# Twenty-eight key tiles turned beside the even layer: each load, its turning passes and its store pinned to one projection unit

## The chip, the cores and the metric

The kernel runs on one core of one Trainium2 chip. The metric is the device time of one execution in microseconds (us). The engines named below are TensorE (PE: matmuls; PEld: its weight loads), VectorE (DVE), ScalarE (ACT), GpSimd (POOL) and SyncE (SP). SP computes nothing: it issues nearly all transfers (DMAs), one after the other, in the order of its queue, and holds the queue while an issue waits for a semaphore.

## The reference, cut to what matters

One inference step of two layers, for a prompt of 2048 tokens and for 8 sample sequences of 4 tokens, each with 2048 cached tokens in pages of 128 rows:

```python
def even_mixer(h, w_in, ...):
    proj = h @ w_in                                   # all of the even layer's projections
    qa, fa, ia, ga, qb, kb, vb, gb, fb = _split(proj, ...)
    o_a, s_a = gated_linear_chunked(...)              # HGRN2 heads (group A)
    o_b = fox_attend(hb(qb), kb_h, vb_h, log_fb)      # forgetting attention (group B)
    return jnp.concatenate([o_a * silu(ga), o_b * silu(gb)], -1) @ w_out, ...

def fox_sample(q, k, v, log_f, k_pages, v_pages, logf_pages, page_table):
    k_past = k_pages[page_table].reshape(db, -1, H, dh)    # 128 pages of 128 x 4 x 128, f32
    logit_past = einsum('bthd,bshd->bhts', q, k_past) * scale + ...
    ...
```

The odd layer (GLA) and a final norm follow. `logit_past` needs the cached keys with the head dimension on the partitions, so every key page has to be turned before TensorE can use it.

## The kernel before, in words

The even layer is one long run of 32 projection units, `us[0]` to `us[31]`: 16 blocks of columns of `w_in` for the first half of the prompt, and the same 16 for the second half. A unit is a chain of matmuls (L629 to L631: each product is done as three f16 matmuls of high and low parts), the eviction of the results by ScalarE and VectorE, and stores by SP. Beside the units run four linear-attention heads per half (`lin(h)`, tiles `qA`, `kA`, `gl_A`). `staged` walks through a unit's steps, and prepares the weights of the units one to three ahead: load (`wr_...`), largest absolute value (`rm_...`, L306), scale (`pow_...`, `kc`), split in f16 parts (`w_...`, L360).

At the second and the fourth step of a unit (`n in (1, 3)`), `staged` calls `beside(2 * j + n // 2)`, and that calls `ahead`. `ahead` prepares `PRE = 28` of the 32 tiles of cached keys. A tile takes:

- four loads of 256 KB, `kp<-in_cache_fox_k`, L1528 on SP, ahead of which SP reads the four page numbers into registers (L1520: a TENSOR_LOAD and eight short instructions);
- four turning passes of VectorE, `kT<-kp`, L1532, STREAM_TRANSPOSE of 128x512 f32;
- one store of 1 MB, `kT<-kT`, L1548 on SP, into a scratch tensor in DRAM.

The last four tiles are turned later, in the fox phase, which also reads the 28 back (`ktd<-kT`, L1592) for the scores of the samples (`sc`, L1692). The fox phase follows the 32 units directly: its first VectorE instruction is L1418 (`L<-s,cm`).

The order on each engine is not the order of this code. The program is recorded, and a scheduler then puts each engine's instructions in a row by its own timetable: an instruction that has its inputs and its buffer by that timetable may stand far ahead of where it is written. A block `with tc.issue_after(ins)` adds an edge: whatever is recorded in it for the engine of `ins` stands behind `ins` in that engine's row. Edges set only the row; on the chip every engine works through its row strictly, and waits at an instruction until its semaphores are there. In the kernel before, a tile's loads have an edge to the loads of the tile before (`last_page`), and the turning passes have none.

Tile buffers: `lr` (two) up to unit 15, `wr` (three, shared with raw weights) from then on. Each tile uses one for `kp` and one for the turned tile.

## Time and profile before

| | |
|---|---|
| median of 3 runs | 2357.52 us (2351.48 to 2358.5) |
| profiled execution | 2351.95 us; its span (first to last instruction) 2350.3 us |
| busy, share of the span | PE 95%, PEld 67%, DVE 59%, ACT 42%, POOL 31% |
| mean granted TensorE clock | 0.978 |
| turning passes L1532 in the even layer | 112, from 45.7 to 639.3 us, 70.2 us busy |
| fox phase's first L1418 on VectorE | 936.3 us |

The span is 1.65 us shorter than the profiled execution's time, and that execution is 5.6 us under the median. "Granted clock" is the share of TensorE's full speed that the chip gave in a stretch; the records show 1.0 and 0.5 in turns, and a row gives the mean. DMA share is the mean busy share of 16 DMA engines and can be a little over 1. "Idle before" in a row is the time the engine stood still just ahead of these instructions, and the name behind the arrow is what ended it.

### The profile page before, as it was taken

The numbers are of one execution on the slowest core, as the hardware profiler recorded it, in microseconds if no ns is written. First come the engines' busy times: TensorE is split into PE (matmuls) and PEld (weight loads), VectorE is DVE, ScalarE is ACT, GpSimd is POOL, SyncE is SP. The second block draws the span as 40 slices with busy tenths as digits, with TensorE's granted clock in tenths as the row PEclk, the third lists the DMA queues.
The fourth block names the chain that finished last, engine by engine and source line by source line (L and its number), as shares of the span: only waits on it lengthen the run. The fifth ranks groups of instructions, "written<-read, shape, count | busy, mean of one in ns | idle before, by whom it ended". The sixth has DMA issues, their size and how long they took to land.

```text
span 2350.3 us, 58071 instructions
## 1 busy us (share of the span) xinstructions
PE 2221.6 (95%) x23316; PEld 1581.5 (67%) x23316; DVE 1395.6 (59%) x3138; ACT 992.1 (42%) x2200; POOL 731.1 (31%) x788
## 2 busy tenths in 40 slices
PE   6988999899899999898999999999999999999998
PEld 5556767785365578564545888777677666666887
DVE  5865566843654455758677635356665655547554
ACT  5322434411022122546566543546545535545343
POOL 1232234200110111524345536144452432322233
PEclk9999999999899999999999999999999999999999
DMA  8878335899954135998784978523233532115554
GB/s 220 257 217 271 110 101 173 275 283 271 281 163 145 60 124 158 353 321 234 236 271 154 325 223 253 144 91 109 80 118 76 129 103 63 44 60 162 162 182 157
DMA packets 367600, 420.65 MB, mean 179 GB/s; under 512 B 108785, under 2 KB 303666, under 8 KB 356066
## 3 DMA queue, kind: packets, MB, share of 16 engines
q1 hardware_dynamic: 365186, 410.32, 57.3%
q0 software_dynamic: 2144, 6.62, 0.8%
q8 instruction: 183, 3.00, 0.5%
q14 instruction: 87, 0.71, 0.1%
HBM read 274.16 MB, written 125.78 MB: 170 GB/s over the span
## 4 chain that ended last, share of the span: by engine, by line
PE 46%; DVE 4%; DMA 2%; ACT 2%; issue 2%; POOL 2%; SPq 1%; POOLq 0%; DVEq 0%; ACTq 0%
PE pt_o L629 4%; PE pt_o L630 4%; PE pt_o L631 4%; PE pt L1454 2%; PE pt_Cv L631 2%; PE pt_Cv L629 2%; PE pt_Cv L630 2%; PE pv L1772 1%; PE o_C L913 1%; PE fo L629 1%; PE gl_C L760 1%; PE fo L630 1%; PE fo L631 1%; PE s L629 1%; PE sc L1692 1%
## 5 line engine op out<-in xcount | busy, mean ns | idle before, releaser
L629 PE MATMUL pt_o<-w_o,act 128*128 128x256 f16 x1024 | 278.9, 273 | 1.1 <-ACT sg1C L686 1.1
L630 PE MATMUL pt_o<-w_o,act 128*128 128x256 f16 x1024 | 278.9, 273 | 0.0
L631 PE MATMUL pt_o<-w_o,act 128*128 128x256 f16 x1024 | 278.7, 273 | 0.0
L629 PEld LDWEIGHTS <-act 128*128 128x128 f16 x2304 | 227.4, 99 | 41.8 <-DVE Bvs L1074 6.0
L630 PEld LDWEIGHTS <-act 128*128 128x128 f16 x2304 | 227.4, 99 | 34.4 <-issue 4.7
L631 PEld LDWEIGHTS <-act 128*128 128x128 f16 x2304 | 227.2, 99 | 30.9 <-issue 2.0
L793 POOL TENSOR_TENSOR kA<-kA,fA 128x512 f32<-128x512 f32 (+1 forms) x56 | 76.6, 1368 | 404.7 <-PE gl_A L760 323.0
L629 PE MATMUL pt_Cv<-w_Cv,act 128*128 128x256 f16 (+1 forms) x512 | 141.4, 276 | 0.0
L631 PE MATMUL pt_Cv<-w_Cv,act 128*128 128x256 f16 (+1 forms) x512 | 141.3, 276 | 0.0
L630 PE MATMUL pt_Cv<-w_Cv,act 128*128 128x256 f16 (+1 forms) x512 | 141.2, 276 | 0.0
L1426 ACT ACTIVATE L<-L,nm,kc 128x512 f32<-128x512 f32 (+3 forms) x160 | 118.2, 740 | 44.8 <-DVE nm L1424 42.7
L1532 DVE STREAM_TRANSPOSE kT<-kp 128x512 f32<-128x512 f32 x112 | 70.2, 681 | 105.8 <-DMA kp<-in_cache_fox_k 99.3
L1461 ACT ACTIVATE th<-pt 128x512 f16<-128x512 f32 (+3 forms) x159 | 81.0, 527 | 110.2 <-PE pt L1454 109.3
L1434 POOL TENSOR_SCALAR L<-L,nm 128x512 f32<-128x512 f32 (+3 forms) x160 | 100.3, 642 | 86.8 <-DVE nm L1430 45.2
L793 POOL TENSOR_TENSOR kC<-kC,fC 128x512 f32<-128x512 f32 (+1 forms) x56 | 80.4, 1437 | 139.7 <-PE gl_C L760 94.1
L1462 DVE TENSOR_TENSOR tl<-pt,th 128x512 f16<-128x512 f32 (+3 forms) x159 | 94.7, 607 | 27.8 <-ACT th L1461 25.9
L1454 PE MATMUL pt<-ident,L 128*128 128x128 f32 x544 | 89.3, 278 | 4.4 <-DVE tl L1462 2.6
L1454 PEld LDWEIGHTS pt<-ident,L 128*128 128x128 f32 x544 | 64.4, 142 | 32.5 <-DVE tl L1462 9.8
L792 DVE TENSOR_TENSOR qC<-qC,fC 128x512 f32<-128x512 f32 (+1 forms) x56 | 72.9, 1302 | 22.0 <-PE gl_C L760 22.0
L1972 ACT ACTIVATE vC<-pt_Cv,kc 128x512 f32<-128x512 f32 (+1 forms) x40 | 23.9, 599 | 135.1 <-PE pt_Cv L631 135.1
L629 PE MATMUL pt_Bv<-w_Bv,act 128*128 128x260 f16 (+1 forms) x256 | 71.5, 279 | 6.1 <-DVE Bvs L1074 2.4
L629 PE MATMUL pt_Bk<-w_Bk,act 128*128 128x256 f16 x256 | 71.0, 277 | 2.8 <-DVE Bvs L1074 2.8
(961 smaller groups left out, 6475.8 us busy)
## 6 DMA issues: line engine op xcount, KB each, us to landing
pgcache_fox_v<-in_cache_fox_v SPq DMA_DIRECT2D x128, 256.0 KB, 4.5
kp<-in_cache_fox_k SPq DMA_DIRECT2D x112, 256.0 KB, 6.9
kT<-kT SPq DMA_DIRECT2D x28, 1024.0 KB, 5.2
ktd<-kT SPq DMA_DIRECT2D x28, 1024.0 KB, 10.6
yr<-yT SPq DMA_DIRECT2D x16, 1024.0 KB, 7.2
x1d<-xo SPq DMA_DIRECT2D x44, 256.0 KB, 4.7
wr_o<-in_w_out_even SPq DMA_DIRECT2D x32, 256.0 KB, 5.5
xo<-in_x_prompt SPq DMA_DIRECT2D x32, 256.0 KB, 5.0
```

Of the source, the lines that this page charges most:

```text
L629: nc.tensor.matmul(ps, lh[0], rh[0], start=first, stop=False)
L630: nc.tensor.matmul(ps, lh[0], rh[1], start=False, stop=False)
L631: return nc.tensor.matmul(ps, lh[1], rh[0], start=False, stop=last)
L792: nc.vector.tensor_tensor(xv[:, :, 1], xv[:, :, 1], t0.to_broadcast([P, nb, w]), ALU.mult)
L793: nc.gpsimd.tensor_tensor(kv[:, :, 0], kv[:, :, 0], t1.to_broadcast([P, nb, w]), ALU.mult)
L1426: self.last_exp = nc.scalar.activation(lt[:, :w], lt[:, :w], AF.Exp, bias=nm[:, 0:1], scale=ib, accum_out=nm[:, 2 + j : 3 + j])
L1434: nc.gpsimd.tensor_scalar(lt[:, :w], lt[:, :w], nm[:, 1:2], 2.0**14, ALU.mult, ALU.mult)
L1454: nc.tensor.transpose(pt[:, w : w + P], rows[b][s // 4][0][:, (s % 4) * P : (s % 4 + 1) * P], self.ident)
L1461: nc.scalar.activation(th[:, a:w], pt[:, a:w], AF.Copy),
L1462: nc.vector.tensor_tensor(tl[:, a:w], pt[:, a:w], th[:, a:w], ALU.subtract)))
L1532: return self.nc.vector.transpose(kt[:, :, 32 * x : 32 * x + 32], t[:, x].rearrange("p (a e) -> p a e", e=32))
L1972: r = nc.scalar.activation(v[h][:, g : g + cnt], ps[:, :, :256], AF.Copy, scale=c)
```

## The change

The call of `ahead` moves from `beside` into `staged`, and is made with the unit and its step. For the tile m = u - 4 of unit u:

- step 1: read the page numbers and issue the four loads, with an edge to `last_sp`, the last transfer that was recorded by then;
- step 3: three of the four passes, with an edge to `last_dve`, the last VectorE instruction of some kinds that was recorded by then;
- next unit, step 0: the fourth pass, with the same kind of edge;
- next unit, step 1: the store, ahead of the next tile's loads.

The two names are kept up to date by assignments in the functions that issue transfers and evictions, which change nothing else. `PRE0` changes from 8 to 4 because it now counts units and not half units.

```diff
-PRE0 = 8
+PRE0 = 4
...
-                    nc.sync.dma_start(ydst[t][:, dcol : dcol + w], y[:, :w])
+                    self.last_sp = nc.sync.dma_start(ydst[t][:, dcol : dcol + w], y[:, :w])
...
             def beside(x):
-                self.ahead(wpool, x)
                 x -= 33
...
-            self.ahead(wpool, 64)
+            for n in range(2):
+                self.ahead(wpool, 32, n)
...
-                if beside and n in (1, 3):
-                    beside(2 * j + n // 2)
+                if beside:
+                    self.ahead(self.wpool, j, n)
+                    if n in (1, 3):
+                        beside(2 * j + n // 2)
...
+    def ahead(self, pool, u, n):
+        nc, m = self.nc, u - PRE0
+
+        def turns(xs):
+            with self.tc.issue_after(self.last_dve.ins):
+                for x in xs:
+                    self.turn_block(self.kt_ahead, self.kp_ahead, x)
+
+        if n == 0 and 0 < m <= PRE:
+            turns([3])
+        if n == 1 and 0 < m <= PRE:
+            nc.sync.dma_start(self.kT[m - 1], self.kt_ahead.rearrange("p a s -> p (a s)"))
+        if not 0 <= m < PRE:
+            return
+        tag = "lr" if u < 16 else "wr"
+        if n == 1:
+            self.kp_ahead = pool.tile([P, 4, 512], F32, tag=tag, name=f"kp{m}")
+            with self.tc.issue_after(self.last_sp.ins):
+                regs = self.page_regs(m % 2, m // 2)
                 for x in range(4):
+                    self.page_load(self.kp_ahead, "cache_fox_k", regs[x], x)
+        if n == 3:
+            self.kt_ahead = pool.tile([P, NH * 4, P], F32, tag=tag, name=f"kt{m}")
+            turns(range(3))
```

What this does to the rows of the engines, at three places. The turned tile is called kT before and kt now. First, VectorE where the first half's activations are prepared (`act`, `nt`); `rm_Ag` and `pow_Ag` belong to the weights of the second unit. Before:

```order
L625 SCALAR_TENSOR_TENSOR act_121<-nt512_7_416,g_even_65,act_121 128x256
L306 TENSOR_REDUCE rm_Ag00_472<-wr_Ag00_366 128x1 x4
L1532 STREAM_TRANSPOSE kT0_2005<-kp0_1856 128x16x32 x4
L625 SCALAR_TENSOR_TENSOR act_121<-nt768_0_478,g_even_65,act_121 128x256
L625 SCALAR_TENSOR_TENSOR act_121<-nt768_1_483,g_even_65,act_121 128x256
```

And now:

```order
L625 SCALAR_TENSOR_TENSOR act_121<-nt512_7_416,g_even_65,act_121 128x256
L306 TENSOR_REDUCE rm_Ag00_472<-wr_Ag00_366 128x1 x4
L625 SCALAR_TENSOR_TENSOR act_121<-nt768_0_478,g_even_65,act_121 128x256
L625 SCALAR_TENSOR_TENSOR act_121<-nt768_1_483,g_even_65,act_121 128x256
L625 SCALAR_TENSOR_TENSOR act_121<-nt768_2_488,g_even_65,act_121 128x256
```

The first tile's passes have left this place; they now stand in unit 4, behind evictions of the tile `Bq`. The eleven tiles behind it have moved back in the same way.

Second, SP at the second place, near the end of the first half, where the units B store their rows (`vd`, `out_fox_v_p`). Before:

```order
L398 DMA lr_o03_7277<-in_w_out_even 128x2x256 x4
L1548 DMA kT_85<-kT13_7141 128x2048
L1088 DMA vd0_74<-Bvs000_5528 128x2x512
L1528 ISA
L1528 DMA kp14_7222<-in_cache_fox_k 32x4x512
```

And now:

```order
L1549 DMA kT_85<-kt8_5442 128x2048
L1088 DMA vd0_74<-Bvs000_5527 128x2x512
L1522 TENSOR_LOAD scTs0_880
L1522 ISA x8
L1530 ISA
L1530 DMA kp9_5585<-in_cache_fox_k 32x4x512
```

The loads of tile 9 stand where those of tile 14 stood, so five fewer tiles have been moved by this time. VectorE's row for the same tile, ahead of which stand the second half's activations (`xhl`), now reads:

```order
L528 TENSOR_TENSOR xhl_6208<-ny640_6205,xhl_6208 128x1024
L532 SCALAR_TENSOR_TENSOR xhl_6334<-ny768_6330,rsr_n768_6341,xhl_6334 128x1024
L1534 STREAM_TRANSPOSE kt9_5725<-kp9_5585 128x16x32 x3
L1059 SCALAR_TENSOR_TENSOR lf_891<-pt_Bv004_5735,kc_67,bfox_814 128x4
L1067 TENSOR_SCALAR Bv004_5761<-pt_Bv004_5735,kc_67 128x256
```

Before, passes of tile 14 stood a few instructions further on. Third, VectorE at the end of the 32 units, where the last eviction (`Bvs`) is followed by the fox phase. Before:

```order
L1074 SCALAR_TENSOR_TENSOR Bvs116_11830<-pt_Bv116_11780,kc_67,Bvs116_11830 128x2x128
L275 TENSOR_REDUCE kc_67<-vmax_68 128x1
L1074 SCALAR_TENSOR_TENSOR Bvs116_11830<-pt_Bv116_11780,kc_67,Bvs116_11830 128x2x128
L1418 ISA L000_11889,mx00_11884<-s000_11885,cm00_11882 128x128
L1418 ISA mx00_11884 128x1
```

And now:

```order
L1074 SCALAR_TENSOR_TENSOR Bvs116_11830<-pt_Bv116_11780,kc_67,Bvs116_11830 128x2x128
L275 TENSOR_REDUCE kc_67<-vmax_68 128x1
L1074 SCALAR_TENSOR_TENSOR Bvs116_11830<-pt_Bv116_11780,kc_67,Bvs116_11830 128x2x128
L1534 STREAM_TRANSPOSE kt27_11839<-kp27_11679 128x16x32 x4
L1420 ISA L000_11889,mx00_11884<-s000_11885,cm00_11882 128x128
```

All four passes of the last tile now stand ahead of the fox phase's first instruction; before, they stood about 300 us earlier. On SP the four loads of that tile now stand right behind the store of `Bvs112`:

```order
L1088 DMA vd1_75<-Bvs112_11669 128x2x512
L1522 TENSOR_LOAD scTs0_880
L1522 ISA x8
L1530 ISA
L1530 DMA kp27_11679<-in_cache_fox_k 32x4x512
```

More of the change, by code (lines that the diff above doesn't have):

```diff
@@ L340, in fetch @@
                 with nc.allow_non_contiguous_dma(reason="a few columns"):
-                    nc.sync.dma_start(t["raw"][:, a * h : (a + 1) * h, off : off + n], src)
+                    self.last_sp = nc.sync.dma_start(t["raw"][:, a * h : (a + 1) * h, off : off + n], src)
         def parts():
@@ L384, in load @@
             t["w"] = Parts(self.w_tile(pool, nm, width))
-            self.nc.sync.dma_start(t["w"].both.rearrange("p x k c -> p (x k c)"), kept[:, : 2 * KT * width])
+            self.last_sp = self.nc.sync.dma_start(t["w"].both.rearrange("p x k c -> p (x k c)"), kept[:, : 2 * KT * width])
         return lambda: None, load, lambda: None, lambda: t["w"]
@@ L742, in out @@
                                         for z in (yo, gate))
-                        nc.vector.scalar_tensor_tensor(yo, src, gain[:, t : t + 1], gate, ALU.mult, ALU.mult)
-                    nc.sync.dma_start(ydst[t][:, dcol : dcol + w], y[:, :w])
+                        self.last_dve = nc.vector.scalar_tensor_tensor(yo, src, gain[:, t : t + 1], gate, ALU.mult, ALU.mult)
+                    self.last_sp = nc.sync.dma_start(ydst[t][:, dcol : dcol + w], y[:, :w])
             return out
@@ L793, in levels @@
                 nc.gpsimd.tensor_tensor(kv[:, :, 0], kv[:, :, 0], t1.to_broadcast([P, nb, w]), ALU.mult)
-                nc.vector.tensor_tensor(t1, t1, t0, ALU.mult)
+                self.last_dve = nc.vector.tensor_tensor(t1, t1, t0, ALU.mult)
         def decode():
@@ L1001, in run @@
                                         ALU.mult, ALU.add)
-                nc.vector.tensor_scalar(f[h][:, :n], f[h][:, :n], self.fb[:, h : h + 1], self.fa[:, h : h + 1],
+                self.last_dve = nc.vector.tensor_scalar(f[h][:, :n], f[h][:, :n], self.fb[:, h : h + 1], self.fa[:, h : h + 1],
                                         ALU.mult, ALU.add)
@@ L1013, in store_cols @@
                 if lo < hi:
-                    nc.sync.dma_start(dst[:, dc + lo - a : dc + hi - a], t[:, lo - c0 : hi - c0])
+                    self.last_sp = nc.sync.dma_start(dst[:, dc + lo - a : dc + hi - a], t[:, lo - c0 : hi - c0])
         def mk_bq(hp, which):
@@ L1028, in ev @@
                             nc.scalar.activation(u[:, 0], ps[:, : m - few], AF.Copy, scale=up)
-                            nc.vector.scalar_tensor_tensor(u[:, 1], ps[:, : m - few], up, u[:, 0], ALU.mult,
+                            self.last_dve = nc.vector.scalar_tensor_tensor(u[:, 1], ps[:, : m - few], up, u[:, 0], ALU.mult,
                                                            ALU.subtract)
                             dc = hf * HALF + c0
-                            nc.sync.dma_start(self.qd[h][:, :, dc : dc + m - few], u)
+                            self.last_sp = nc.sync.dma_start(self.qd[h][:, :, dc : dc + m - few], u)
                             if few:
@@ L1073, in ev @@
                             nc.scalar.activation(hi, src, AF.Copy, scale=self.cu[which, hp])
-                            nc.vector.scalar_tensor_tensor(lo, src, self.cu[which, hp], hi, ALU.mult, ALU.subtract)
+                            self.last_dve = nc.vector.scalar_tensor_tensor(lo, src, self.cu[which, hp], hi, ALU.mult, ALU.subtract)
                     if m < P:
@@ L1532, in turn_block @@
         return self.nc.vector.transpose(kt[:, :, 32 * x : 32 * x + 32], t[:, x].rearrange("p (a e) -> p a e", e=32))
-    def ahead(self, pool, y):
-        y -= PRE0
-        if y % 2:
-            if y // 2 < PRE and y > 0:
-                t, tag = self.key
-                self.key = pool.tile([P, NH * 4, P], F32, tag=tag, name=f"kT{y // 2}"), y // 2
-                for x in range(4):
-                    self.turn_block(self.key[0], t, x)
-            return
-        n = y // 2
-        if 0 < n <= PRE:
-            kt, m = self.key
-            self.nc.sync.dma_start(self.kT[m], kt.rearrange("p a s -> p (a s)"))
-        if 0 <= n < PRE:
-            tag = "lr" if y + PRE0 < 32 else "wr"
-            t = pool.tile([P, 4, 512], F32, tag=tag, name=f"kp{n}")
-            with ExitStack() as st:
-                if n:
-                    st.enter_context(self.tc.issue_after(self.last_page.ins))
-                regs = self.page_regs(n % 2, n // 2)
-            for x in range(4):
-                self.last_page = self.page_load(t, "cache_fox_k", regs[x], x)
-            self.key = t, tag
+    def ahead(self, pool, u, n):
[15 more added lines that the diff above has]
+                regs = self.page_regs(m % 2, m // 2)
+                for x in range(4):
+                    self.page_load(self.kp_ahead, "cache_fox_k", regs[x], x)
+        if n == 3:
+            self.kt_ahead = pool.tile([P, NH * 4, P], F32, tag=tag, name=f"kt{m}")
+            turns(range(3))
     def fox_sample(self, fs, pps):
```

6 lines of the change are left out of this document (3 added, 3 removed).

## The prediction

> **What bounds the kernel now.** I read the page's first table, then the time by stretches of the even layer, then who waited for whom in the bad stretches, and last two stalls instruction by instruction.
>
> ```profile
> PE 2221.6 (95%) x23316; PEld 1581.5 (67%) x23316; DVE 1395.6 (59%) x3138; ACT 992.1 (42%) x2200; POOL 731.1 (31%) x788
> ```
>
> TensorE is the bound; what can be gained is its idle time and the time at half clock. The next view has the busy time of each engine in a stretch, then granted clock, DMA share and GB/s.
>
> ```profile
> core 0: us, PE busy (x) PEld busy (x) DVE busy (x) ACT busy (x) POOL busy (x), PEclk, DMA share, GB/s
> 40.00:240.00 200.00, 172.09 (x1948) 117.52 (x1947) 133.41 (x303) 63.91 (x145) 50.72 (x52) 0.92 0.81 235
> 240.00:430.00 190.00, 184.90 (x2187) 134.47 (x2185) 116.94 (x256) 80.69 (x184) 68.35 (x52) 0.98 0.44 140
> 430.00:660.00 230.00, 204.80 (x1744) 133.47 (x1742) 124.77 (x282) 43.07 (x95) 17.99 (x14) 0.93 0.99 280
> 660.00:920.00 260.00, 258.55 (x2952) 179.91 (x2951) 139.32 (x327) 62.95 (x174) 39.82 (x37) 1.00 0.36 114
> ```
>
> All this is the same kind of work, the projection units. Yet TensorE is idle for 27.9 us of the first stretch and 25.2 us of the third, and for only 5.1 and 1.5 us of the other two; the clock and the DMA share part in the same way. Which work stands in the bad stretches? The groups of VectorE instructions in those two windows, first in each list:
>
> ```profile
> L1532 DVE STREAM_TRANSPOSE kT<-kp 128x512 f32<-128x512 f32 x48 | 30.2, 682 | 33.9 <-DMA kp<-in_cache_fox_k 32.4 <-DMA qs<-BqS 1.4
> L1532 DVE STREAM_TRANSPOSE kT<-kp 128x512 f32<-128x512 f32 x60 | 37.6, 681 | 71.9 <-DMA kp<-in_cache_fox_k 66.9 <-issue 5.0
> ```
>
> That is 108 of the 112 passes, and VectorE stood still for 33.9 and 71.9 us at the head of one. They wait for their own loads. Whether TensorE pays is told by its waits in the first window, and in the third:
>
> ```profile
> PE nt L483 <- DVE act L625: 6.7, 1, 6.7
> PE pf_Bq L629 <- DVE Bq L1029: 4.1, 1, 4.1
> PE pS_Av L674 <- DVE sam_Av L669: 4.1, 1, 4.1
> PE oS_A L825 <- DVE scTs L785: 2.6, 1, 2.6
> PE spr_Ag L293 <- ACT BqS L1035: 2.3, 1, 2.3
> PE gl_A L760 <- DVE qA L714: 1.8, 1, 1.8
> ```
>
> ```profile
> PE gl_A L760 <- DVE qA L714: 5.1, 1, 5.1
> PE gl_A L760 <- DVE qA L792: 3.5, 1, 3.5
> PE pf_A10f L629 <- DVE pow_o L295: 2.7, 1, 2.7
> PE pt_Bv L629 <- DVE Bvs L1074: 2.4, 2, 2.0
> PE pt_Bv L629 <- DVE kc L278: 2.1, 1, 2.1
> PE gl_A L760 <- DVE kc L285: 1.7, 1, 1.7
> PE pf_A11f L629 <- DVE pow_o L295: 1.3, 1, 1.3
> ```
>
> None of these names a key tile, since TensorE waits for what is queued behind the pass. Two stalls show the link (VectorE, then TensorE; in brackets the idle time before):
>
> ```profile
> 45.68 2.49 DVE L1532 STREAM_TRANSPOSE kT<-kp 128x512 f32<-128x512 f32 x4 [5.34 <-DMA kp<-in_cache_fox_k]
> 48.10 1.62 DVE L625 SCALAR_TENSOR_TENSOR act<-nt,g_even,act 128x256 f16<-128x256 f32 x4
> ...
> 48.59 1.97 PE L483 MATMUL nt<-ident,nx 128*128 128x128 f32 x8 [6.74 <-DVE act L625]
> ```
>
> ```profile
> 598.53 2.49 DVE L1532 STREAM_TRANSPOSE kT<-kp 128x512 f32<-128x512 f32 x4 [3.53 <-DMA kp<-in_cache_fox_k]
> ...
> 601.37 1.22 DVE L714 TENSOR_TENSOR qA<-qA,fA 128x1024 f32<-128x1024 f32 x1
> ...
> 602.64 1.06 PE L760 MATMUL gl_A<-qA,kA 128*32 128x16 f32 x64 [5.11 <-DVE qA L714]
> ```
>
> In the first, VectorE is held 5.34 us by the load and 2.49 us by the passes, and TensorE stands for 6.74 us. I put all the waits listed above down to the passes, taking 2.0 of the 2.4 us of `Bvs`: 21.6 us in the first stretch and 18.4 us in the third, 40.0 us.
>
> **The change, part by part.**
>
> 1. The 48 passes ahead of 240 us and most of those up to 660 us leave VectorE's early row; 28 tiles are spread over units 4 to 31. The passes' own work (70.2 us on an engine 59% busy) stays and lies beside TensorE's. What goes is the waiting: **-40.0 us** of TensorE idle.
>
> 2. The clock. In the stretch without the passes, 240 to 430 us, it is 0.98, in the two bad ones 0.92 and 0.93. Lost work: 0.06 x 172.09 + 0.05 x 204.80 = **-20.5 us**. The records show how it comes: after the 2.6 us stall at `scTs`, TensorE ran at half speed for a whole stretch,
>
> ```profile
> 223.00:229.80 6.80, 6.60 (x83) 4.71 (x72) 4.50 (x9) 0.75 (x4) 5.04 (x5) 0.50 1.00 317
> ```
>
> The Trainium skill ("TensorE: Matmul & The Clock Gate", section "HAM oscillation — how this bites in real kernels") makes the rule that TensorE should have no idle gap over about 3.4 us, and costs each such gap 1.7 us. By it only the five stalls of 3.5 to 6.7 us would cost clock, an estimate of 8.5 us in place of 20.5. The row above speaks against it as a threshold for this kernel: half speed after 2.6 us.
>
> 3. What waits at the new places. A pass now stands behind an eviction of its own unit, and its loads one or two steps ahead. The loads' landing time is
>
> ```profile
> DMA to landing us min/median/max: 3.3/6.9/10.9
> ```
>
> I took, for each tile, the times that the instructions ahead of its loads (SP) and of its first pass (VectorE) have in this trace. The first and the worst-placed of the ordinary tiles: tile 0's loads stand behind stores issued up to 163.6 us, its passes behind `Bq` at 182.4, and nothing waits:
>
> ```profile
> 163.63 0.60 SPq L744 DMA_DIRECT2D yT<-y_A00S  x1
> ...
> 182.37 0.58 DVE L1029 SCALAR_TENSOR_TENSOR Bq<-pf_Bq,kc,Bq 128x352 f16<-128x352 f32 x1
> ```
>
> Tile 9:
>
> ```profile
> 443.89 0.56 SPq L1088 DMA_DIRECT2D vd<-Bvs  x1
> ...
> 452.99 1.28 DVE L532 SCALAR_TENSOR_TENSOR xhl<-ny,rsr_n,xhl 128x1024 f16<-128x1024 f32 x1
> ```
>
> Its four loads would go out from about 445 to 449 (2.81 us for three of four in today's row) and land about 456, some 2 to 5 us after 454.3, when VectorE is free. By such laying-over, 19 tiles have their data in time and eight lack 1 to 5 us, together about 18 us (my estimate). A ninth, tile 12, lacks about 18 us at the change of halves, but there the trace shows a wait of that kind that cost nothing: VectorE stood 23.49 us while TensorE had work.
>
> ```profile
> 543.68 2.49 DVE L1532 STREAM_TRANSPOSE kT<-kp 128x512 f32<-128x512 f32 x4 [23.49 <-DMA kp<-in_cache_fox_k]
> ```
>
> Leaving that one out, today's 33.9 + 71.9 - 23.5 = 82.3 us of waiting cost 40.0 us of idle TensorE, a rate of 0.49, and 20.5 us of clock, 0.25. So 18 us cost **+9 and +4.5 us**. Bounds: nothing, if all is absorbed; or every tile short by the median landing time, 28 x 6.9 x 0.74 = 143 us. I take 13.5, nearer the low end, because 19 of 28 have their data in time.
>
> 4. The handover. The last tile is now turned between the last `Bvs` and the fox phase's first VectorE instruction, and TensorE already waits there:
>
> ```profile
> 926.60 4.96 SPq L1088 DMA_DIRECT2D vd<-Bvs  x2
> 935.93 0.48 DVE L1074 SCALAR_TENSOR_TENSOR Bvs<-pt_Bv,kc,Bvs 128x256 f16<-128x256 f32 x1 [0.47 <-ACT Bvs L1073]
> 936.33 0.28 DVE L1418 CUSTOM_DVE_ANT_0 L<-s,cm 128x128 f32<-128x128 f32 x1
> ```
>
> ```profile
> PE s L629 <- DVE mx L1418: 3.1, 3, 2.7
> ```
>
> The loads go out behind the first of the two `vd` stores, about 928 to 931, and land about 938, so 1.5 us of waiting and 2.5 us of passes (the row at 45.68) ahead of L1418, and the store behind them holds SP's next loads: **+5 us** (low 2.5, the passes alone; high 9, at the longest landing).
>
> 5. SP. The number of transfers is the same. The stores now stand behind a pass of the next unit; SP is held for the pass, and behind it queue weight loads that run one to three units ahead, which hides a few us. The page reads (nine short instructions) now stand in a busy queue instead of an idle one; for them I take nothing, with the weights' lead as cover. If that cover is gone, a weight lands late by the same few us. The early weights and activations gain, as the loads and stores of twelve tiles no longer compete with them ahead of 240 us; for this I take nothing either, and rival B is its bound.
>
> Sum: -40.0 - 20.5 + 13.5 + 5 = **-42 us**. Against the profiled execution that is 2351.95 - 42 = 2310 us; the median of the runs shown is 5.6 us above that execution, so I say 2357.5 - 42 = 2315.5, rounded 2316 us.
>
> **The rivals.**
>
> A. The saturated stretch stays as it is. From 430 to 660 us the DMA engines are 0.99 busy, and 7 or 8 tiles still move there; TensorE's stalls could pass to other late transfers. Then only the first stretch gains: -21.6 - 10.3 + 18.5 = -13 us, 2344 us. For it: the DMA share. Against: the waits there name evictions, not transfers.
>
> B. More is gained, as the early stretches become like 660 to 920 us: idle 0.6% and clock 1.00. That is 53.1 - 2.6 of idle and 0.08 x 172.09 + 0.07 x 204.80 = 28.1 of clock, less 5 at the handover: -74 us, 2284 us. Against: all new waits of term 3 would have to be absorbed.
>
> C. Slower: the new places are too close to the loads, and the good stretches, with no slack on TensorE today, become like the bad ones. One mechanism: every tile's first pass waits w us for its own load; cost 28 x w x 0.74. It eats 60.5 - 5 at w = 2.7 us, and from there on the kernel is slower; at w = 3.5 it takes 2375 us. For it: the scheduler places by its own timetable, not by the landing times here. Against: the 19 tiles.
>
> D. The clock follows the skill's rule ("TensorE: Matmul & The Clock Gate", as above); worked out from rows: half speed only after the five stalls of 3.5 us and more, each for one 3.4 us record (half of the 6.80 us row), so 5 x 1.7 = 8.5 us gained in place of 20.5: -30 us, 2328 us. Against: the 223 us row.
>
> E. No difference: TensorE is held at the same places by the linear attention's chain, and waits as long for it as it did for the passes; 2357 us. For it: the chain's names, `qA` and `gl_A`, in the waits. Against: the pairs of rows above.
>
> That the change does not do what it says is excluded by the rows of the engines.
>
> **How the numbers follow.** Forecast 0.47 (its own range 2298 to 2334), A 0.20, B 0.12, C 0.09, D 0.05, E 0.07. This kernel's runs differ by 0.3% (7 us), so that is what counts as no change. Faster: 0.47 + 0.20 + 0.12 + 0.05 = 0.84; same 0.07; slower 0.09. The range leaves out C, E and the far side of B: 2284 to 2350 us.
>
> **What would show it.** Right: no wait of L1532 ahead of 160 us; TensorE idle under 12 us of each of the two bad stretches, and clock 0.96 or more there; waits of L1532 under 40 us in all, the longest near the change of halves; L1418 starting 2.5 to 9 us after the last `Bvs`; everything behind it as long as before. Wrong: waits of L1532 over 75 us in all, or new stalls of TensorE between units 4 and 16 or after unit 20, would make it C; waits that now name weights (`w_`, `kc`) in the second half would make it A.

## The result, and the profile after

The changed kernel takes 2323.3 us (median of 4 runs, 2315.94 to 2329.01), the kernel before 2358.01 us (4 runs on the same chip, 2351.48 to 2359.21): ratio 0.9857, 95% interval 0.9823 to 0.9891. It is faster, by about 34 us (1.4%). The profiled execution of the changed kernel took 2315.94 us, 36.0 us less than that of before; the readings below are of these two executions.

The view by stretches, with the columns of the prediction (length; busy time and instructions of each engine; granted clock, DMA share, GB/s):

```profile
40.00:240.00 200.00, 195.34 (x2258) 140.59 (x2257) 137.48 (x317) 82.15 (x194) 63.23 (x60) 1.00 0.52 157
240.00:430.00 190.00, 177.92 (x2154) 132.13 (x2153) 132.28 (x287) 76.04 (x172) 60.59 (x50) 0.97 0.64 198
430.00:660.00 230.00, 219.03 (x2242) 142.90 (x2240) 126.44 (x278) 44.94 (x102) 20.07 (x15) 0.99 0.88 250
660.00:920.00 260.00, 234.44 (x2352) 160.29 (x2350) 144.83 (x353) 57.29 (x155) 41.35 (x57) 0.95 0.65 193
```

TensorE's idle time falls from 27.9 to 4.7 us in the first stretch and from 25.2 to 11.0 us in the third; the clock there rises to 1.00 and 0.99. The two good stretches have become worse: 5.1 to 12.1 us, and 1.5 to 25.6 us. The last one now contains the handover to the fox phase, which came 45 us later before; three stalls there (8.29, 3.99 and 5.51 us) make up 17.8 of the 25.6 us.

The group of the turning passes, and the landing times of their loads:

```profile
L1534 DVE STREAM_TRANSPOSE kt<-kp 128x512 f32<-128x512 f32 x112 | 72.1, 684 | 55.0 <-DMA kp<-in_cache_fox_k 50.6 <-DMA ny<-in_x_prompt 4.3
```

```profile
DMA to landing us min/median/max: 3.1/5.2/9.6
```

The waits at the passes are halved (105.8 us before), not gone, and a load's median landing falls from 6.9 to 5.2 us. Where the remaining waits cost time can be read in the timeline (start, length, engine, line; idle time ahead in brackets), at the change of halves and in the second half:

```profile
505.47 1.90 DVE L1534 STREAM_TRANSPOSE kt<-kp 128x512 f32<-128x512 f32 x3 [21.40 <-DMA kp<-in_cache_fox_k]
...
510.81 0.15 DVE L308 TENSOR_REDUCE rm_o<-rm_o 128x1 f32<-128x4 f32 x1
...
511.11 0.70 PE L293 MATMUL spr_o<-ident,rm_o 128*128 128x128 f32 x2 [4.60 <-DVE rm_o L308]
...
791.14 1.90 DVE L1534 STREAM_TRANSPOSE kt<-kp 128x512 f32<-128x512 f32 x3 [7.21 <-DMA kp<-in_cache_fox_k]
...
793.18 0.71 DVE L792 TENSOR_TENSOR qA<-qA,fA 128x512 f32<-128x512 f32 x1
...
794.03 0.82 PE L760 MATMUL gl_A<-qA,kA 128*32 128x16 f32 x64 [3.15 <-DVE qA L792]
```

The pair is the same as before: VectorE held by a load, and TensorE by what stands behind the pass.

To see where time was won and lost I matched the n-th matmul of each name in both traces and subtracted the start times. This "lead" is 37.7 us at the 384th `pt_Av` (212.5 us now, 250.2 before), 46.7 at the last `pt_Bv` of the first half (469.0 against 515.7), 35.1 at 518 us, behind the change of halves, 57.0 at 618 us, 45.3 at the last projection matmul (887.9 against 933.2), 32.5 at the last `s` of the fox phase (1245.8 against 1278.3), 36.0 at the end. So the change lost 11.6 us at the change of halves, 11.7 late in the second half, and 12.8 at the handover.

### The profile page after: what moved, and what is told of

Its sections match the earlier page's. It is cut to its first block, busy times and chain, and to the rows that moved or that the text cites. A ratio compares the mean times of both kernels' runs of the same rounds, so it can differ in the third digit from the quotient of the medians.

```text
span 2314.2 us, 58064 instructions
## 1 busy us (share of the span) xinstructions
PE 2197.3 (95%) x23316; PEld 1571.4 (68%) x23316; DVE 1405.8 (61%) x3138; ACT 991.5 (43%) x2200; POOL 727.3 (31%) x788
## 4 chain that ended last, share of the span: by engine, by line
PE 69%; DMA 10%; DVE 8%; SPq 4%; issue 4%; ACT 3%; POOL 2%; POOLq 0%; DVEq 0%; ACTq 0%
PE pt_o L629 4%; PE pt_o L630 4%; PE pt_o L631 4%; PE pt_Cv L629 2%; PE pt_Cv L631 2%; PE pt_Cv L630 2%; PE pt L1456 2%; DMA kp<-in_cache_fox_k 2%; DMA ny<-in_x_prompt 1%; PE gl_A L760 1%; PE o_C L913 1%; PE gl_C L760 1%; SPq L1522 1%; PE pt_Bk L629 1%; PE fo L629 1%
## 5 line engine op out<-in xcount | busy, mean ns | idle before, releaser
L1534 DVE STREAM_TRANSPOSE kt<-kp 128x512 f32<-128x512 f32 x112 | 72.1, 684 | 55.0 <-DMA kp<-in_cache_fox_k 50.6
L629 PE MATMUL s<-k,q 128*128 128x512 f16 (+3 forms) x160 | 57.0, 356 | 23.3 <-DVE mx L1420 8.8
L629 PE MATMUL pt_Av<-w_Ai,act 128*128 128x256 f16 x256 | 71.6, 280 | 3.4 <-DVE few_Bv L679 3.2
```

The lines of the kernel that those rows point to most:

```text
L629: nc.tensor.matmul(ps, lh[0], rh[0], start=first, stop=False)
L1534: return self.nc.vector.transpose(kt[:, :, 32 * x : 32 * x + 32], t[:, x].rearrange("p (a e) -> p a e", e=32))
```

## The experiments

Three theories of the gain stood against each other. W: it is the waits at the passes, as predicted. T: it is the traffic, since 48 of the 112 loads are issued by 240 us in the kernel before, and 16 in the changed one (the expectations call this theory S or, from e9 on, theory 1). H: what the change could gain is larger, and is lost again at the handover and through the new edges. Four quantities are given for each kernel: loads issued by 240 us, idle time of VectorE ahead of the passes, ratio to the kernel before with its interval, and the lead at four of these places (384th `pt_Av`; last `pt_Bv` of the first half; last projection matmul; last `s` of the fox phase). The counts and leads are of one profiled execution each, the ratios of all runs; the profiled execution of e1 was 5 us over its kernel's median and that of e7 10 us, so a few us between two leads decide nothing.

| kernel | loads by 240 us | waits at passes | ratio | lead, us |
|---|---|---|---|---|
| before | 48 | 105.8 | 1 | 0, 0, 0, 0 |
| changed | 16 | 55.0 | 0.9857 (0.9823 to 0.9891) | 37.7, 46.7, 45.3, 32.5 |
| e1 | 20 | 56.0 | 0.9837 (0.9814 to 0.9860) | 34.1, 38.9, 34.4, 28.9 |
| e2 | 20 | 171.1 | 1.0001 (0.9986 to 1.0016) | 30.3, 24.5, 11.6, 2.5 |
| e3 | 16 | 26.7 | 0.9792 (0.9755 to 0.9829) | 38.8, 51.1, 61.0, 51.2 |
| e4 | 48 | 69.1 | 0.9938 (0.9921 to 0.9956) | 9.5, -8.2, 8.6, 15.4 |
| e5 | 48 | no passes | 0.9850 (0.9813 to 0.9887) | 19.8, 3.0, 26.6, 34.3 |
| e6 | 20 | 25.9 | 0.9777 (0.9740 to 0.9813) | 35.7, 48.9, 57.0, 56.2 |
| e7 | 20 | 7.5 | 0.9708 (0.9672 to 0.9745) | 37.3, 43.3, 58.8, 60.3 |
| e8 | 16 | 53.9 | 0.9848 (0.9808 to 0.9887) | 38.0, 47.1, 44.8, 36.6 |
| e9 | 24 | no passes | 0.9825 (0.9790 to 0.9860) | 32.5, 32.9, 41.5, 37.1 |
| e10 | 52 | no passes | 0.9875 (0.9839 to 0.9910) | 13.7, -4.2, 19.4, 24.2 |
| e11 | 20 | 17.1 | 0.9744 (0.9710 to 0.9778) | 37.3, 39.1, 52.7, 52.8 |
| e12 | 24 | no passes | 0.9858 (0.9831 to 0.9885) | 33.3, 31.5, 30.8, 27.6 |

**e1, all one unit earlier.** The tile m goes to unit m + 3, so that the last one is turned a unit ahead of the fox phase.

```diff
-PRE0 = 4
+PRE0 = 3
```

> The changed kernel with the whole chain one unit earlier (tile m in unit m + 3), so that the last tile is turned and stored before the last unit and nothing of it stands at the handover to the fox phase. Theory H (the last tile holds up the handover): the lead over the kernel before, 45.3 us at the last projection and 32.6 us after the fox phase, is kept, so 2323 - 13 = about 2310 us (2304 to 2316); L1420 starts within 1 us of the last Bvs and the half-clock stretch of 20.5 us from 893 us on shrinks to 10 us or less. Rival (the handover is late because the fox phase's own loads are late): 2323 us, within 4.

Measured: 2318.39 us, 0.9837, between the two expected ranges. The lead lost between the last projection matmul and the end of the fox phase is 5.5 us in place of 12.8. The profiled execution shows 10.9 us less lead ahead of that, but it was the longest of its four, and against the changed kernel nothing is resolved.

**e2, only the loads pinned.** The passes have no edge, and the scheduler places them by its own timetable; the loads keep the change's edge.

```diff
-            with self.tc.issue_after(self.last_dve.ins):
-                for x in xs:
-                    self.turn_block(self.kt_ahead, self.kp_ahead, x)
+            for x in xs:
+                self.turn_block(self.kt_ahead, self.kp_ahead, x)
```

> The changed kernel, but only the loads have an edge; the passes stand where the scheduler puts them. Theory W (what costs is VectorE standing at a pass for its own load): the passes stand closer behind their loads than in the changed kernel, waits of L1532 or its like of 60 to 90 us, and the time lies between the two, 2325 to 2345 us. Rival S (what helps is that the traffic is spread, and no longer bunched ahead of 240 us): the loads are as spread as in the changed kernel, so 2323 us, within 5, whatever VectorE waits.

Measured: 2353.45 us (10 runs), no gain: slower than either theory expected, and with about twice the waiting that W expected. The group, and one of its waits in the timeline:

```profile
L1534 DVE STREAM_TRANSPOSE kt<-kp 128x512 f32<-128x512 f32 x112 | 70.1, 681 | 171.1 <-DMA kp<-in_cache_fox_k 155.7 <-DMA lr_Cv<-in_w_in_odd 11.4 <-DMA sgd<-Bg 4.0
```

```profile
581.92 2.49 DVE L1534 STREAM_TRANSPOSE kt<-kp 128x512 f32<-128x512 f32 x4 [13.05 <-DMA kp<-in_cache_fox_k]
...
584.55 0.71 DVE L792 TENSOR_TENSOR qA<-qA,fA 128x512 f32<-128x512 f32 x1
...
585.40 0.80 PE L760 MATMUL gl_A<-qA,kA 128*32 128x16 f32 x45 [5.85 <-DVE qA L792]
```

Left alone, the passes go up close behind their loads and wait more than in the kernel before. The spread of the loads is nearly the changed kernel's, and its early lead of 30 us is lost again, piece by piece. Spread loads without placed passes are worth nothing here.

**e3, only the passes pinned.** The loads have their old edge (to the loads of the tile before) in place of the one to SP's last transfer.

```diff
-            with self.tc.issue_after(self.last_sp.ins):
-                regs = self.page_regs(m % 2, m // 2)
...
+            with ExitStack() as st:
+                if m:
+                    st.enter_context(self.tc.issue_after(self.last_page.ins))
+                regs = self.page_regs(m % 2, m // 2)
...
```

> The changed kernel, but only the passes have an edge; the loads stand where the scheduler puts them (behind the loads of the tile before). Two buffers hold a tile's loads back until the passes of the tile before are done, so they spread by themselves, some a little earlier. Theory W: waits for loads as in the changed kernel or fewer (30 to 50 us), 2315 to 2325 us. Rival (each of the two edges is needed): half of the gain is lost, 2335 to 2345 us.

Measured: 2302.97 us, 0.9792, faster than either range expected; the waits are halved once more:

```profile
L1534 DVE STREAM_TRANSPOSE kt<-kp 128x512 f32<-128x512 f32 x112 | 72.2, 684 | 26.7 <-DMA kp<-in_cache_fox_k 26.7
```

The loads spread all the same: 16 of them are issued by 240 us, as in the changed kernel (in e10, with this edge and without passes, 52). So here it is the placed passes that hold the loads back, and the edge of the loads gives no further spread but more waiting. The two ratios differ by 0.0065, 15 us, though their intervals just overlap.

**e4, passes that read a tile which is ready.** The kernel before, where the passes read a tile filled once at the start (the stored keys are then wrong ones, and so are the samples' scores).

```diff
+            self.still = sp.tile([P, 512], F32, name="still")
+            nc.gpsimd.memset(self.still, 0.25)
...
-                    self.turn_block(self.key[0], t, x)
+                    self.nc.vector.transpose(self.key[0][:, :, 32 * x : 32 * x + 32],
+                                             self.still.rearrange("p (a e) -> p a e", e=32))
```

> The kernel before, but the 112 passes read a tile that is ready from the start, not the loaded keys (the samples' scores are then of wrong keys); all loads, passes and stores are made, as early and as bunched as before. Theory W: TensorE's idle time goes with VectorE's waits, 2358 - 45 = about 2313 us (2300 to 2325), and what is left of VectorE's waits at L1532's passes is for stores, under 25 us. Rival S (the bunched traffic is what costs): no gain, 2358 us within 7; a mixture would lie between.

Measured: 2340.03 us, 0.9938, between the ranges of the two theories. It didn't take the waits away:

```profile
L1545 DVE STREAM_TRANSPOSE kT<-still 128x512 f32<-128x512 f32 x112 | 70.9, 681 | 69.1 <-DMA kp<-in_cache_fox_k 48.4 <-DMA kT<-kT 16.4 <-issue 4.0
```

The passes no longer need the loads' data, yet most of what they wait for is still named as a load, which leaves the shared buffers; the run does not decide.

**e5, the kernel before without its passes.** Loads and stores stay, and a store carries the unturned tile (the turning is left out, and the samples' scores are taken of unturned keys). A tile then takes one buffer in place of two.

```diff
-                t, tag = self.key
-                self.key = pool.tile([P, NH * 4, P], F32, tag=tag, name=f"kT{y // 2}"), y // 2
-                for x in range(4):
-                    self.turn_block(self.key[0], t, x)
+                self.key = self.key[0], y // 2
```

> The kernel before without the 112 turning passes: the stores carry the loaded tiles unturned (the samples' scores are then of unturned keys). All loads and stores are made, 12 tiles of them ahead of 240 us as before; VectorE has nothing left to wait for. In the run with the ready tile it still waited 69 us at the passes, since the turned tiles' buffers were those of loads under way, so this is the clean test. Theory W (VectorE's waits at the passes cost TensorE 40 us of idle and 20 of clock): 2355 - 50 = about 2305 us (2290 to 2320). Rival S (the early bunched traffic costs): 2355 us, within 7. Half of each: 2330 us.

Measured: 2314.87 us, 0.985, in the range of theory W, and 35 us of 2350. With no pass left to wait, two of the stretches still show:

```profile
40.00:240.00 200.00, 182.04 (x2137) 129.27 (x2135) 117.95 (x278) 73.92 (x172) 57.51 (x56) 0.97 0.83 245
...
430.00:660.00 230.00, 211.73 (x1937) 139.07 (x1936) 103.75 (x237) 49.40 (x117) 19.46 (x17) 0.96 0.90 261
```

TensorE idles 18.0 and 18.3 us in the two stretches that the prediction called bad because of the passes, and the clock stays at 0.97 and 0.96. So the passes, their waits, their work and their second buffers were worth 35 us together, and not the 60.5 that the prediction put down to the waits alone: 0.33 us per us of waiting (35 / 105.8), net, with the early transfers left in place. The idle time that is left stands at other places than before. These are TensorE's longest waits in the two stretches:

```profile
PE spr_Aqf L293 <- ACT sg L686: 5.2, 1, 5.2
PE pf_Ag L629 <- ACT sg L686: 4.7, 1, 4.7
PE spr_Ag L293 <- ACT BqS L1035: 2.6, 1, 2.6
```

```profile
PE pt_Bv L629 <- DVE Bvs L1074: 8.9, 2, 6.1
PE pt_Bk L629 <- DVE Bvs L1074: 4.9, 1, 4.9
```

Of the 40.0 us listed in the prediction, the waits for `act`, `Bq`, `scTs` and `pow_o` and all four of `gl_A`, 29.5 us together, are gone; those for `BqS` and `Bvs` are not. What has come in their place stands behind transfers that are late: the first wait, in the timeline, behind the load of weights `wr_Bq`,

```profile
70.06 0.69 DVE L306 TENSOR_REDUCE rm_Bq<-wr_Bq 128x1 f32<-128x512 f32 x1 [10.38 <-DMA wr_Bq<-in_w_in_even]
...
74.94 0.80 PE L293 MATMUL spr_Aqf<-ident,rm_Aqf 128*128 128x128 f32 x2 [5.22 <-ACT sg L686]
```

and the wait of 4.86 us at 454.48 behind 4.66 us in which ScalarE waited for `ny`. SP's queue is held too, for 27.6 us in all, by stores that wait for their own loads.

**e6, e3 and e1 together.** The loads with their old edge as in e3, and `PRE0 = 3` as in e1.

> Only the passes have an edge (as in the run that gained most), and the whole chain is one unit earlier, so that the last tile is turned before the last unit. Theory H: that run had a lead of 61.0 us at the last projection and of 51.2 us after the fox phase; the 10 us are the last tile's, and most are kept: 2303 - 8 = about 2295 us (2289 to 2299). Rival (the shift only moves the loss elsewhere, as it did by 9 of 12 us when the changed kernel was shifted): 2300 to 2306 us.

Measured: 2297.65 us, 0.9777, clear of the changed kernel's interval and as theory H expects. Between last projection and end of the fox phase only 0.8 us of lead is lost.

```profile
L1534 DVE STREAM_TRANSPOSE kt<-kp 128x512 f32<-128x512 f32 x112 | 72.4, 684 | 25.9 <-DMA kp<-in_cache_fox_k 25.9
```

**e7, and the passes a step later.** As e6, with all four passes at the next unit's step 0 and the store at its step 2, so that a tile's loads have two to three steps to land.

```diff
         if n == 0 and 0 < m <= PRE:
-            turns([3])
-        if n == 1 and 0 < m <= PRE:
+            self.kt_ahead = pool.tile([P, NH * 4, P], F32, ...)
+            turns(range(4))
+        if n == 2 and 0 < m <= PRE:
             nc.sync.dma_start(self.kT[m - 1], ...)
...
-        if n == 3:
-            self.kt_ahead = pool.tile([P, NH * 4, P], F32, tag=tag, name=f"kt{m}")
-            turns(range(3))
```

> As the run before this one, but all four passes of a tile stand in the next unit's first step and the store in its third, so that a load has about one step more to land. Theory W: VectorE's waits for loads, 26.7 us in the run with pinned passes, fall under 8 us, and at 0.74 us of time for one of waiting the kernel takes another 10 us less: about 2287 us (2280 to 2294). Rival (the waits that are left are at places where TensorE has work): no difference to the run before this one, within 4 us.

Measured: 2283.87 us, 0.9708, in the range of theory W: the fastest of all, about 69 us faster than before and about 35 faster than the changed kernel by the ratios (its profiled execution, 2294.36 us, was the longest of its four). Against e6 it is 16 us by the ratios, with intervals that just overlap. The group and the stretches:

```profile
L1534 DVE STREAM_TRANSPOSE kt<-kp 128x512 f32<-128x512 f32 x112 | 69.7, 676 | 7.5 <-DMA kp<-in_cache_fox_k 7.4
```

```profile
40.00:240.00 200.00, 195.33 (x2259) 140.64 (x2257) 137.61 (x318) 82.69 (x194) 62.84 (x60) 1.00 0.55 165
240.00:430.00 190.00, 180.52 (x2128) 133.03 (x2127) 133.45 (x287) 75.79 (x172) 64.38 (x51) 0.94 0.64 201
430.00:660.00 230.00, 225.18 (x2296) 147.51 (x2294) 134.08 (x290) 47.26 (x106) 21.66 (x16) 0.99 0.88 251
660.00:920.00 260.00, 246.00 (x2563) 168.33 (x2561) 155.31 (x399) 68.32 (x185) 54.65 (x91) 0.97 0.70 217
```

The gain over the changed kernel stands in the third and fourth row, where the waits of 505, 791 and 832 us and those of the handover were. What is left of waits at the second half's start is for weights (`rm_o` for `lr_o`, 29.5 us of VectorE in the even layer). In the second row the clock is 0.94, lower than before: stalls of 2.3 and 3.2 us behind `scTs` are left there.

**e8, 27 tiles.** The changed kernel without the tile that stands at the handover; the fox phase turns five tiles in place of four.

```diff
-PRE = 28
+PRE = 27
```

> The changed kernel with PRE = 27: the last tile is left to the fox phase, which turns five tiles in place of four. Theory H: the handover is freed, L1420 starts within 1 us of the last Bvs, the 17 us that the lead lost between the last projection and the samples' first scores shrink to 5, and the fifth tile in the fox phase costs 2 to 4 us: about 2314 us (2309 to 2319). Rival (the fox phase's own loads are what is late there): 2323 us or a little more.

Measured: 2315.97 us, 0.9848; the time is in the range of theory H, but the ratio is not resolved from the changed kernel's. From the last projection matmul to the first `sc` 5.6 us of lead are lost, in place of the changed kernel's 17.3, and to the end of the fox phase, which now includes a fifth tile, 8.2 in place of 12.8. The last tile's place is what costs there: up to the first `sc` the other two kernels with that tile at the handover, e2 and e3, lose 13.5 and 11.7 us, and those that have it a unit earlier (e1, e6, e7 and e9 to e12) 0.2 to 5.2. e6 shows that the loss can be saved by moving everything a unit ahead. One stall of the handover stays in e8, TensorE's wait ahead of its first `s`:

```profile
PE s L629 <- DMA sgs<-sgd: 7.8, 1, 7.8
```

**e9, e10, e12: spread transfers without passes.** What e5 leaves open is whether the transfers' place is worth the rest of e7's gain. Three runs tried to show it. All leave out the turning, and the samples' scores are of unturned keys. e9: the changed kernel a unit earlier, passes gone, the store of the loaded tile at the next unit's step 1.

```diff
-            turns([3])
...
-            nc.sync.dma_start(self.kT[m - 1], self.kt_ahead.rearrange("p a s -> p (a s)"))
+            nc.sync.dma_start(self.kT[m - 1], self.kp_ahead.rearrange("p a s -> p (a s)"))
...
-            self.kt_ahead = pool.tile([P, NH * 4, P], F32, tag=tag, name=f"kt{m}")
-            turns(range(3))
```

> The changed kernel with the tiles one unit earlier, the loads spread one to a unit as there, but no turning passes: each store carries the tile as it was loaded, so VectorE never waits for a load (left out: the turning, and so the samples' scores are taken of unturned keys). Beside the run without passes whose loads and stores are bunched early (2314.87 us, 0.985): theory 1, the spread of the loads and stores is worth as much as the waits, expects the change of halves not to lose the 17 us that the bunched one lost there, TensorE idle under 10 us in each of the stretches to 660 us, and 2283 us (2272 to 2292), ratio about 0.970. Theory 2, the waits are all and the place of the traffic is free, expects the same as the bunched run without passes, 2315 us (2307 to 2322), ratio about 0.985.

e10: the kernel of e7, passes gone.

```diff
-            self.kt_ahead = pool.tile([P, NH * 4, P], F32, ...)
-            turns(range(4))
+            self.kt_ahead = self.kp_ahead
```

> The version with the passes a step later (2283.87 us, 0.9708), without its turning passes: the same spread of tiles, the loads' old edge, and each store, at the same place, carries the tile as it was loaded (left out: the turning; the samples' scores are taken of unturned keys). Beside the run without passes whose transfers are bunched early (0.985). Theory 1, the place of the transfers is worth about 30 us and passes with ample lead cost nothing: the same as with the passes, 2284 us (2276 to 2292), ratio 0.971. Theory 2, the place of the transfers is free and the gain of that version came from elsewhere: as the bunched run, 2315 us (2307 to 2322), ratio 0.985. In the first run of this kind (0.9825) SyncE's queue was held for 80.8 us by the stores, which waited there for their loads; here they have a unit's lead, and it should be held under 20 us.

e12: the same as e10, but with the changed kernel's edge for the loads (`with self.tc.issue_after(self.last_sp.ins)` around the page reads and loads, as in the diff of the change).

> The run before the last in this study let the loads go early again (52 of 112 issued by 240 us, against 20 in the version with passes), since nothing holds them when the passes are gone: it is a second bunched run (0.9875), not a spread one. Here the loads are held by the edge to SyncE's last issued transfer, and the stores, without passes, have a step more than in the first spread run, so that they do not hold the queue. It is the run of 2296.22 us (0.9744) without its passes (left out: the turning; the samples' scores are taken of unturned keys). Expected with 20 to 24 loads by 240 us. Theory 1, the spread is what gains, and passes with lead cost nothing: 2294 us (2284 to 2303), ratio 0.974. Theory 2, the place of the transfers is free: as the bunched ones, 2315 to 2325 us, ratio 0.985 to 0.9875. A third, the passes themselves (70 us of VectorE) still cost: 2275 us or less, ratio below 0.967.

Measured: 2312.52 (0.9825), 2325.06 (0.9875) and 2323.07 us (0.9858): e9 and e12 in the range of the theory that the place of the transfers is free, e10 above both of its ranges. First the stretch to 240 us in e9, e10 and e12:

```profile
40.00:240.00 200.00, 193.13 (x2225) 138.86 (x2224) 128.29 (x297) 80.71 (x191) 58.88 (x58) 0.98 0.58 176
```

```profile
40.00:240.00 200.00, 178.82 (x2091) 126.46 (x2090) 114.96 (x273) 71.22 (x160) 55.92 (x55) 0.93 0.84 251
```

```profile
40.00:240.00 200.00, 192.95 (x2233) 138.98 (x2232) 128.94 (x301) 81.28 (x192) 58.71 (x59) 0.99 0.58 176
```

With the passes gone nothing held e10's loads back, and they went early, 52 of them by 240 us: it is a second run of e5's kind, and as slow. e9 and e12 did spread. In this stretch, without any pass in the four kernels, the spread ones leave TensorE 6.9 and 7.0 us idle, the bunched ones 18.0 (e5) and 21.2; the lead at the 384th `pt_Av` is 32.5 and 33.3 against 19.8 and 13.7 us. So the early transfers cost 13 to 20 us there (32.5 - 19.8 to 33.3 - 13.7). e2 agrees: it has its passes, which wait 18.4 us up to that matmul, but spread loads, and leads there by 30.3 us, 10 more than e5 without any such wait. Its stretch, and its passes up to 219.8 us:

```profile
40.00:240.00 200.00, 188.41 (x2192) 134.51 (x2190) 130.63 (x305) 74.83 (x175) 55.72 (x56) 0.99 0.53 161
```

```profile
L1534 DVE STREAM_TRANSPOSE kt<-kp 128x512 f32<-128x512 f32 x16 | 10.0, 680 | 18.4 <-DMA kp<-in_cache_fox_k 14.4 <-DMA sgd<-Bg 4.0
```

Behind the first stretch the two spread runs without passes lose by another way, in the waits of SP's queue (e9, then e12):

```profile
SPq L1547 <- DMA kp<-in_cache_fox_k: 80.8, 37, 5.3
```

```profile
SPq L1544 <- DMA kp<-in_cache_fox_k: 86.2, 38, 5.8
```

The stores stand a few issues behind their own loads, and now SP waits in place of VectorE, with weights and the units' stores queued behind it. So what a clean spread without passes is worth in the whole kernel stays open: e9 and e12 have the time expected if the place of the transfers is free, but with a new wait that e7 does not have.

**e11, e7 with the changed kernel's edge for the loads.** The edit is that of e12, with the passes left in.

> The version with the passes a step later, but with the change's edge for the loads (all behind SyncE's last issued store or load) in place of the old one. Before: the edge cost 20 us with the passes of the change (2323 against 2303). If the edge itself costs (it holds the loads back, and what is queued behind them), about 2300 us (2293 to 2310), ratio 0.978. If it cost only because the passes stood too close behind their loads, nothing here: 2284 us (2277 to 2291), ratio 0.971, and waits of the passes under 15 us.

Measured: 2296.22 us, 0.9744. It is 0.0036 (8 us) from e7, with overlapping intervals, between the two ratios expected (by the time in the range of the first); the waits at the passes are 17.1 us, not 7.5:

```profile
L1534 DVE STREAM_TRANSPOSE kt<-kp 128x512 f32<-128x512 f32 x112 | 69.8, 678 | 17.1 <-DMA kp<-in_cache_fox_k 17.1
```

That is the direction of e3 against the changed kernel again, with a smaller size where the passes have more lead.

## Why the prediction was right, and where its terms were not

The forecast of 2316 us lies 7 us under the median of 2323.3; the sum was -42 us, the profiled executions differ by -36.0. The likeliest case was the one that came: both bad stretches improved, and it is not the slower kernel of C. Of its signs, no pass waits ahead of 160 us (the first waits at 179.75, for 2.59 us), the idle times and clocks of the two bad stretches are as said, and L1420 starts 5.4 us after the start of the last `Bvs`. One sign of C did appear, new stalls between units 4 and 16 and after unit 20 (4.60 us at 363, 3.15 at 794, 2.75 at 835), but with a cost too small to undo the gain. Up to the last projection matmul the terms expect -60.5 + 13.5 = -47 us, and the lead there is 45.3. But the sum is right in part by errors that offset each other.

**Terms 1 and 2, waits and clock, -60.5 us.** All the waits listed for the bad stretches, and the whole loss of clock, were put down to the waiting of the passes. e5, which takes the passes away and leaves the transfers, shows 35 us. The step that failed is "I put all the waits listed above down to the passes", in two ways. I took all rows for held by a pass because two pairs showed that; for 29.5 of the 40.0 us e5 bears it out, but the rows of `BqS` and `Bvs` stay when the passes go. And a stall taken away was counted as time gained: in e5, with no pass to hold it, TensorE still idles 36 us in these stretches, of 53 before, largely at new or longer stalls, of which those followed up stand behind late transfers. That is what rival A feared for the saturated stretch. With it goes the one rate of 0.74 us per us of waiting: e5 gives 0.33 with the transfers left bunched, and pairs of kernels that both spread them give 0.3 (e2 against the changed kernel, 34 us for 116.1) and 0.9 (e6 against e7, 16 us for 18.4, hardly resolved).

**Term 5, nothing for the traffic.** That offsets the first error. e7 has 98.3 us less waiting than before, worth 32 us at 0.33, and gained 69; the other 37 us is my estimate of what the spread of loads and stores brings, of which e5 and e10 against e9 and e12 show 13 to 20 us, in the first stretch. The two numbers together give for the changed kernel 0.33 x 50.8 + 37 - 12.8 (the handover) = 41 us, where about 34 was measured, for e2 37 - 0.33 x 65.3 - 9 (its handover, 11.6 to 2.5) = 6, where nothing was, and for e3 0.33 x 79.1 + 37 - 9.8 = 53, where 49 was. In the same way e1, e6, e8 and e11 come out at 48, 63, 46 and 66 us, where 38, 52, 36 and 60 were measured. All are too high, by 4 to 11 us, and for e9 and e12 the same numbers give about 70, where 41 and 33 were measured with SP's queue held. With a higher rate for the waits the 37 us shrink; so only the 13 to 20 us are shown, and the part behind 240 us was not isolated. Rival B named this gain, and its 74 us is close to what e7 reached (69).

**Term 3, new waits.** 55.0 us, where the prediction had about 36 (18 us at eight tiles, another 18 at tile 12) and gave under 40 as the sign; the sign failed, though not as far as the 75 us of rival C. Tile 12's wait was foretold (about 18 us, 21.40 measured) but counted as free. It was not: `rm_o` stood behind it, TensorE waited 4.60 us at 511.11, and between 496 and 518 us 6.6 us of lead went. The step that failed is the row at 543.68, a wait in another place with other work behind it, taken as if its price went with the wait. The new waits ahead of the five stalls at 363, 484, 511, 794 and 835 us (4.30, 6.08, 21.40, 7.21 and 4.91 us, the first of them named as a wait for `ny` and not for keys) cost TensorE 18.3 us of idle time, where the term had 9.

**Term 4, the handover, +5, with bounds of 2.5 and 9.** Measured 12.8 of lead, outside the bounds. The time from the last projection matmul to the first `sc`, before and then after:

```profile
933.20:949.20 16.00, 11.70 (x63) 5.89 (x61) 13.64 (x59) 8.93 (x23) 8.25 (x16) 0.89 0.91 266
```

```profile
887.90:921.20 33.30, 14.43 (x67) 6.75 (x66) 16.85 (x66) 9.39 (x25) 10.00 (x24) 0.69 1.03 279
```

and what stands there now, in the timeline:

```profile
890.49 6.33 SPq L1088 DMA_DIRECT2D vd<-Bvs  x2
...
894.90 0.48 DVE L1074 SCALAR_TENSOR_TENSOR Bvs<-pt_Bv,kc,Bvs 128x256 f16<-128x256 f32 x1 [3.51 <-ACT Bvs L1073]
...
896.51 0.26 PE L629 MATMUL s<-k,q 128*128 128x128 f16 x1 [8.29 <-issue]
...
898.88 2.49 DVE L1534 STREAM_TRANSPOSE kt<-kp 128x512 f32<-128x512 f32 x4 [2.48 <-DMA kp<-in_cache_fox_k]
...
901.40 0.34 SPq L1549 DMA_DIRECT2D kT<-kt  x1
...
901.61 0.48 PE L629 MATMUL s<-k,q 128*128 128x384 f16 x1 [3.99 <-DVE mx L1420]
...
909.04 0.35 DVE L1420 CUSTOM_DVE_ANT_0 L<-s,cm,mx 128x128 f32<-128x128 f32 x1 [5.84 <-POOL cm L1403]
...
909.54 0.59 PE L629 MATMUL s<-k,q 128*128 128x512 f16 x1 [5.51 <-DVE nm L1434]
```

I had counted VectorE's part, 2.48 us of waiting and 2.49 of passes, and that came as said; TensorE's stall of 3.99 us stands behind it. What was missing is what SP does next: the store at 901.40 waits for the passes, SP's next loads for the fox phase are issued behind it, and at 909 us VectorE has stood for 5.84 us and TensorE for 5.51. Neither stall is there in e8, without the last tile. The longest, 8.29 us ahead of the first `s`, is not the tile's, since e8 has it at 7.8 us. SP spends 6.33 us on the two `vd` stores just ahead (4.96 before), but the profile does not name what these 8.29 us waited for, and their cause stays open. About 4.5 of the 17.3 us lost up to the first `sc` comes back by the end of the fox phase.

**Rival D, the clock's rule.** It would not have sized the clock better: by the rows of the two bad stretches (1.00 - 0.92) x 172.09 + (0.99 - 0.93) x 204.80 = 26 us of clock came back there, near the 20.5 us forecast and far from D's 8.5. Nor does the threshold hold. Here are, in the changed kernel, the stretch right behind the 3.15 us stall at 794.03, and that behind a stall of 2.75 us at 834.52:

```profile
794.00:797.50 3.50, 3.47 (x77) 2.69 (x78) 2.96 (x7) 0.95 (x2) 1.50 (x1) 0.57 0.23 76
...
834.40:837.80 3.40, 3.28 (x19) 2.85 (x20) 2.75 (x9) 0.51 (x2) 1.01 (x1) 0.65 0.00 0
```

and in e7, behind one of 2.30 us at 286.17:

```profile
286.10:289.50 3.40, 2.98 (x77) 1.74 (x77) 3.40 (x6) 0.00 (x0) 2.72 (x2) 0.57 0.95 294
289.50:292.90 3.40, 3.40 (x25) 2.36 (x20) 2.57 (x6) 0.37 (x2) 2.68 (x3) 0.50 0.98 330
292.90:296.30 3.40, 3.40 (x13) 1.56 (x11) 0.94 (x3) 0.55 (x1) 1.09 (x2) 0.50 0.65 224
```

The Trainium skill ("TensorE: Matmul & The Clock Gate", section "HAM oscillation — how this bites in real kernels") has as its rule that there should be no idle gap over about 3.4 us; here three shorter ones (3.15, 2.75 and 2.30 us) were each followed by half speed, the last by two whole rows of it and most of a third. The 1.7 us a gap that the prediction names beside this rule are in that section the time at half speed, half of which it counts as lost; that 1.7 us are lost is what a row of 3.4 us at a clock of 0.50 costs here.

## What to carry to other kernels

A consumer that is placed right behind its own transfer on an engine that works in order holds everything queued behind it, so give the load two or three steps of lead and pin the consumer, not the load: pinning the loads alone was worth nothing (1.0001), pinning the passes alone 0.9792, the same a unit earlier 0.9777, and with a step more of lead 0.9708. Before a stall is put down to a wait that stands near it, take the waiting instruction out and see what stays and what comes in its place: two pairs in the trace were right, most of the listed stalls went, and yet the sum over all of them was 1.7 times what came back (60.5 against 35 us). And price a step at a change of phase by every queue it enters, the one that issues the transfers first.

## What the runs showed of the hardware

The amount of transfers in a stretch cost TensorE time without any wait at a pass: at 251 GB/s (e10, 52 early loads) it idled 21.2 us of 200, at 176 GB/s (e9 and e12, 24 early loads) 6.9 and 7.0 us. Whether the DMA engines, the order of SP's queue or the buffers do that was not isolated. And half clock followed a stall of TensorE of only 2.30 us in e7, and lasted for about 10 us; in the kernel before, 6.8 us of it, from 325.4 us on, stand right behind a stall of 1.25 us.
